# Gated linear attention in a two-layer decoder trunk: another sigmoid, one-region sums, half transposes, a second weight pool

## The chip, the cores and the metric

The kernel runs on one core of one Trainium2 chip. The metric is device time in microseconds (us) from launch to end on that core, the median of several runs; before the change three runs gave 2408.81, 2409.51 and 2409.78 us. Engines are named as in the profile: PE is the matrix engine (PEld its weight loads), DVE the vector engine, ACT the scalar engine, POOL the general one, SP the queue that issues the loads.

## What is computed

A decoder trunk of two layers over 272 tokens (16 learned meta tokens, then 256 real ones) with D_MODEL = 2048. Layer 0 mixes tokens with RWKV-7, layer 1 with gated linear attention (GLA); each is followed by an MLP with hidden size 8192. Everything is float32. The change touches layer 1's mixer alone:

```python
def gla_time_mix(x, w_in, w_a2, b_a, gn_w, w_o):        # x: (1, 272, 2048)
    p = x @ w_in                                        # q 1024 | k 1024 | v 2048 | gate 2048 | za 16
    glog = log_sigmoid(za @ w_a2 + b_a) / 16            # forget gate, per key dimension
    # 4 heads, key size 256, value size 512; chunks of 16 (meta) and then 64 tokens:
    #   b = cumsum(glog); q_t = q*exp(b); k_t = k*exp(-b)
    #   o = q_t @ S + tril(q_t @ k_t.T) @ v;  S = exp(b_last)*S + (k*exp(b_last - b)).T @ v
    o = o * rsqrt(mean(o*o, -1) + 1e-5) * gn_w          # per head
    return (o * silu(gate)) @ w_o                       # silu(g) = g * sigmoid(g)
```

## The kernel before

Activations lie transposed: 128 channels on the partitions, tokens along the free dimension. A weight matrix is cut into output tiles of 128 columns; the contraction over 2048 is two weight loads of 128x1024 floats (512 KB each), and each load serves eight steps of 128 (index `kt`, 0 to 15 over both loads). Products are made in three parts of a split float: `wload` (line 127) fetches a load into `raw` (3 buffers, DMA issued by SP), ACT writes its rounded copy `hi` (line 137), DVE the rest `lo = raw - hi` (line 138); `hi` and `lo` have 2 buffers each in the pool `wp`. The activations `x[kt]` have a high and a low half as well.

Two helpers multiply such a tile:

- `proj` (lines 160 to 162 in `mm3`) adds hi·xh, hi·xl and lo·xh for each step into one region of a PSUM bank: three matmuls, the sum is complete in PSUM.
- `projw` (lines 189 and 190) multiplies `hi` with both halves of x in one matmul of 512 columns (two regions of the bank), and `lo` with the high half in a second one of 256 columns. Two matmuls, but two regions are left to be added. `joined` (lines 199, 200) does that for the GLA's tiles: ACT copies one region into `cj`, DVE adds the other. `addto` (line 206) adds both regions into the residual on DVE.

`gla` (from line 987) first multiplies the 16-wide gate input, then runs over four heads. One head's tiles, in the order of PE: two query tiles (`projw` + `joined`, line 1047) and two key tiles (`proj` with 272 tokens, line 1059); then four value tiles (`proj`, line 1114), each transposed into token-major form by three fp32 transposes of 128x128 (line 1123) into one PSUM tile `pt` (2 buffers), copied out as `Vh` (ACT, line 1126) and `Vl` (DVE, line 1127); `weights` (line 1091) makes the chunk scores ahead of the first of them, `weigh(v)` (lines 1103, 1104) multiplies them with the values; then four gate tiles (`projw` + `joined`, line 1139). For each gate tile the sigmoid is made as exp(-g) (ACT, line 1148), plus one (ACT, line 1149), reciprocal (DVE, line 1150); `finish` multiplies it with the normalized output and splits the result into `oT`. A matmul with ones (line 1142) sums the squares for the head's norm behind the second gate tile; during gate tiles 1 and 2 of a head `gate` (line 1017 on PE) prepares the next head's forget gates. After the last head sixteen output tiles (line 1160) multiply `oT` with `gla_o`.

Each engine executes its instructions strictly in the order in which a scheduler wrote them when the program was built; weight loads carry a high priority there (`prio=2000`), so conversions stand as far ahead of their matmuls as the buffers allow. A conversion that waits for a free `hi` holds up all that stands behind it on ACT, and a DVE instruction that waits for ACT holds up the `lo` behind it.

## Time and profile before

| | |
|---|---|
| median of 3 runs | 2409.51 us (2408.81 to 2409.78) |
| profiled execution | 2414.07 us, of it 2412.3 us from the first to the last instruction |
| mean granted PE clock | 0.995 of full speed |
| GLA in the profiled execution | from about 1333 us to the first output tile at 1640 us, output tiles until about 1728 us |
| bytes read from HBM | 433.86 MB |

Times in the profile count from the first instruction. A row of a group of instructions names line, engine, operation, out<-in by the program's names, shape and count, then busy time and the mean of one in ns, then the idle time of that engine just before them and who ended it. In the timeline a row has start and duration; matmuls overlap, so the step between two starts is what one costs, not the duration of one. In a table of stretches each row has the stretch, its length, busy time and instruction count of each engine, the granted PE clock and the DMA share.

### The profile page before, as it was taken

The page shows a single profiled execution, that of the slowest core. Times are in us where ns is not written, and L with a number is a line of the kernel's source. Part 1 is how long each engine was busy: PE and PEld are TensorE (multiplying, and loading weights), DVE is VectorE, ACT ScalarE, POOL GpSimd, SP SyncE. Part 2 cuts the span into 40 slices and gives each one's busy share as a digit, 9 for nine tenths or more (in the row PEclk, how much of TensorE's full clock was granted, in tenths as well). Part 3 has the DMA queues.
Part 4 walks back from the last instruction along what each step waited for, and adds up shares of the span by engine and source line. Part 5 has one row for each costly group of instructions (what it writes and reads, how often), then busy time and mean ns, then how long its engine had stood idle before and what let it go on. Part 6 is the DMA issues. An engine that isn't in the chain of part 4 may idle for free.

```text
span 2412.3 us, 47144 instructions
## 1 busy us (share of the span) xinstructions
PE 2364.2 (98%) x19257; PEld 2233.8 (93%) x19257; DVE 1636.8 (68%) x2742; ACT 1239.3 (51%) x1951; POOL 6.6 (0%) x20
## 2 busy tenths in 40 slices
PE   9999999899999999999999999999999999999998
PEld 8888888789999999999999989998999999999997
DVE  8777886858655555555556788778766666666666
ACT  6366544456555445445445565545555545445444
POOL 0000000000000000000000000000000000000000
PEclk9999999999999999999999999999999999999999
DMA  6578765534555655555555554555666666666665
GB/s 211 170 233 284 240 191 147 148 88 155 183 192 188 190 191 189 188 191 192 187 190 192 182 172 161 166 166 180 197 201 201 201 202 201 202 201 201 201 201 172
DMA packets 160729, 455.29 MB, mean 189 GB/s; under 512 B 34112, under 2 KB 50624, under 8 KB 160512
## 3 DMA queue, kind: packets, MB, share of 16 engines
q1 hardware_dynamic: 160512, 452.27, 58.2%
q8 instruction: 151, 2.47, 0.4%
q14 instruction: 66, 0.54, 0.1%
HBM read 433.86 MB, written 18.35 MB: 187 GB/s over the span
## 4 chain that ended last, share of the span: by engine, by line
PE 70%; DVE 3%; ACT 1%; issue 0%; DVEq 0%; ACTq 0%
PE pj L189 23%; PE pj L160 12%; PE pj L162 12%; PE pj L161 12%; PE pj L190 11%; DVE lo L138 1%; PE pt L1091 0%; DVE sg L1150 0%; ACT hi L137 0%; PE pu L1103 0%; PE pt L1123 0%; DVE cum L1027 0%; DVE fin L1213 0%; PE pu L1104 0%; DVE cj L200 0%
## 5 line engine op out<-in xcount | busy, mean ns | idle before, releaser
L137 ACT CAST hi<-raw 128x1024 fp32r<-128x1024 f32 (+1 forms) x818 | 794.5, 979 | 951.4 <-PE pj L161 514.9
L138 DVE TENSOR_TENSOR lo<-raw,hi 128x1024 fp32r<-128x1024 f32 (+1 forms) x818 | 926.5, 1139 | 518.8 <-ACT hi L137 510.2
L160 PE MATMUL pj<-x,hi 128*128 128x272 f32 x2240 | 642.0, 287 | 5.7 <-DVE cj L200 4.0
L162 PE MATMUL pj<-x,lo 128*128 128x272 f32 x2240 | 629.1, 281 | 4.6 <-DVE lo L138 4.3
L161 PE MATMUL pj<-x,hi 128*128 128x272 f32 x2240 | 628.3, 280 | 0.2 <-DVE x L233 0.2
L189 PE MATMUL pj<-x,hi 128*128 128x512 f32 x1664 | 550.0, 384 | 2.3 <-DVE cj L200 1.3
L190 PE MATMUL pj<-x,lo 128*128 128x256 f32 x1664 | 455.8, 274 | 2.3 <-DVE lo L138 2.2
L160 PEld LDWEIGHTS pj<-x,hi 128*128 128x128 f32 x2240 | 424.2, 189 | 13.7 <-issue 3.7
L162 PEld LDWEIGHTS pj<-x,lo 128*128 128x128 f32 x2240 | 424.4, 189 | 8.0 <-DVE lo L138 7.3
L161 PEld LDWEIGHTS pj<-x,hi 128*128 128x128 f32 x2240 | 424.5, 190 | 3.6 <-issue 1.4
L189 PEld LDWEIGHTS pj<-x,hi 128*128 128x128 f32 x1664 | 315.4, 190 | 46.0 <-ACT hi L137 2.9
L189 PE MATMUL pj<-h,hi 128*128 128x512 f32 x1008 | 330.3, 382 | 0.0
L190 PEld LDWEIGHTS pj<-x,lo 128*128 128x128 f32 x1664 | 320.1, 192 | 6.8 <-DVE lo L138 6.3
L160 PE MATMUL pj<-h,hi 128*128 128x272 f32 (+1 forms) x1040 | 290.1, 279 | 0.0
L161 PE MATMUL pj<-h,hi 128*128 128x272 f32 (+1 forms) x1040 | 290.1, 279 | 0.0
L162 PE MATMUL pj<-h,lo 128*128 128x272 f32 (+1 forms) x1040 | 290.1, 279 | 0.0
L190 PE MATMUL pj<-h,lo 128*128 128x256 f32 x1008 | 274.8, 273 | 0.0
L189 PEld LDWEIGHTS pj<-h,hi 128*128 128x128 f32 x1008 | 190.5, 189 | 26.4
L160 PEld LDWEIGHTS pj<-h,hi 128*128 128x128 f32 x1040 | 196.6, 189 | 0.0
L161 PEld LDWEIGHTS pj<-h,hi 128*128 128x128 f32 x1040 | 196.6, 189 | 0.0
L162 PEld LDWEIGHTS pj<-h,lo 128*128 128x128 f32 x1040 | 196.6, 189 | 0.0
L190 PEld LDWEIGHTS pj<-h,lo 128*128 128x128 f32 x1008 | 193.5, 192 | 0.0
(268 smaller groups left out, 2110.5 us busy)
## 6 DMA issues: line engine op xcount, KB each, us to landing
raw<-mlp_w_d SPq DMA_DIRECT2D x512, 512.0 KB, 4.2
raw<-gla_in_d SPq DMA_DIRECT2D x98, 512.0 KB, 3.4
raw<-w_rkv_d SPq DMA_DIRECT2D x80, 512.0 KB, 4.1
raw<-gla_o_d SPq DMA_DIRECT2D x32, 512.0 KB, 4.2
raw<-w_r_d SPq DMA_DIRECT2D x16, 512.0 KB, 3.4
raw<-rw_oQ_d SPq DMA_DIRECT2D x16, 512.0 KB, 3.4
ard<-ar SPq DMA_DIRECT2D x16, 288.0 KB, 3.6
bkd<-bk SPq DMA_DIRECT2D x16, 288.0 KB, 4.3
```

What stands on the lines that cost most here:

```text
L137: nc.scalar.copy(hi[:, h], raw[:, h])
L138: nc.vector.tensor_tensor(out=lo[:, h], in0=raw[:, h], in1=hi[:, h].bitcast(F32), op=ALU.subtract)
L160: nc.tensor.matmul(out, hi[:, ws], xh, start=first, stop=False)
L161: nc.tensor.matmul(out, hi[:, ws], xl, start=False, stop=False)
L162: nc.tensor.matmul(out, lo[:, ws], xh, start=False, stop=last)
L189: nc.tensor.matmul(wide, hi[:, ws], xt, start=kt == 0, stop=False)
L190: nc.tensor.matmul(one, lo[:, ws], xt[:, 0], start=False, stop=kt == nk - 1)
```

## The change

```diff
@@ Kern.__init__
         self.raw_bufs, self.hi_bufs = 3, 2
         self.split_parts = 1
+        self.wps = [self.wp]
@@ wload
             raw = self.t(self.wp, [P, 1024], "raw", self.raw_bufs)
             nc.sync.dma_start(raw, src)
-            hi = self.t(self.wp, [P, 1024], "hi", self.hi_bufs, F32R)
-            lo = self.t(self.wp, [P, 1024], "lo", self.hi_bufs, F32R)
+            pool = self.wps[0]
+            self.wps = self.wps[1:] + [pool]
+            hi = self.t(pool, [P, 1024], "hi", self.hi_bufs, F32R)
+            lo = self.t(pool, [P, 1024], "lo", self.hi_bufs, F32R)
@@ projw
     def projw(self, srcs, x, off=0):
+        return self.projws([srcs], x, off)[0]
+
+    def projws(self, tiles, x, off=0):
         nc = self.nc
-        ps = self.pj()
-        wide, one = ps.rearrange("p (s t a) -> p s t a", s=2, a=2), self.pairs(ps[:, :SEQ])
-        nk = 8 * len(srcs)
-        for i, s in enumerate(srcs):
-            hi, lo = self.wload(s)
-            for j in range(8):
-                kt = 8 * i + j
-                ws = slice(j * P, (j + 1) * P)
-                xt = x[kt][:, :, off : off + SEQ].rearrange("p s (a t) -> p s t a", a=2)
-                nc.tensor.matmul(wide, hi[:, ws], xt, start=kt == 0, stop=False)
-                nc.tensor.matmul(one, lo[:, ws], xt[:, 0], start=False, stop=kt == nk - 1)
-        return self.back(ps[:, :SEQ]), self.back(ps[:, SEQ:])
+        pss = [self.pj() for _ in tiles]
+        nk = 8 * len(tiles[0])
+        for i in range(len(tiles[0])):
+            for ps, srcs in zip(pss, tiles):
+                wide, one = ps.rearrange("p (s t a) -> p s t a", s=2, a=2), self.pairs(ps[:, :SEQ])
+                hi, lo = self.wload(srcs[i])
+                for j in range(8):
+                    kt = 8 * i + j
+                    ws = slice(j * P, (j + 1) * P)
+                    xt = x[kt][:, :, off : off + SEQ].rearrange("p s (a t) -> p s t a", a=2)
+                    nc.tensor.matmul(wide, hi[:, ws], xt, start=kt == 0, stop=False)
+                    nc.tensor.matmul(one, lo[:, ws], xt[:, 0], start=False, stop=kt == nk - 1)
+        return [(self.back(ps[:, :SEQ]), self.back(ps[:, SEQ:])) for ps in pss]
@@ gla
         gp = es.enter_context(tc.tile_pool(name="gla", bufs=1, side="right", reuse_waits="tile"))
+        self.wps.append(es.enter_context(tc.tile_pool(name="wp2", bufs=1)))
...
-                pq = self.joined(gp, self.projw(pair(j), x, NMETA))
+                pq = self.proj(pair(j), x, SEQ, NMETA)
...
-                pt = self.ptr()
+                pts = [self.ptr(), self.ptr()]
                 for s, a in enumerate((0, c1, c2)):
-                    nc.tensor.transpose(pt[:, s * P : (s + 1) * P], vs[:, a : a + P], self.ident)
-                vc = slice(v * P, (v + 1) * P)
-                p3 = pt[:, : 3 * P].rearrange("p (s v) -> p s v", s=3)
-                nc.scalar.copy(Vh[:, :, vc], p3)
-                tt(Vl[:, :, vc], p3, Vh[:, :, vc].bitcast(F32), ALU.subtract)
+                    for q in range(2):
+                        half = slice(HEAD * q, HEAD * q + HEAD)
+                        nc.tensor.transpose(pts[q][:, s * HEAD : (s + 1) * HEAD], vs[half, a : a + P], self.ident[half, half])
+                for q in range(2):
+                    vc = slice(v * P + HEAD * q, v * P + HEAD * q + HEAD)
+                    p3 = pts[q][:, : 3 * HEAD].rearrange("p (s v) -> p s v", s=3)
+                    nc.scalar.copy(Vh[:, :, vc], p3)
+                    tt(Vl[:, :, vc], p3, Vh[:, :, vc].bitcast(F32), ALU.subtract)
...
-                pg = self.joined(gp, self.projw(pair(32 + 4 * hd + v), x, NMETA))
+                pg = self.proj(pair(32 + 4 * hd + v), x, SEQ, NMETA)
...
                 sg = self.t(gp, [P, SEQ], "sg", 2)
-                nc.scalar.activation(sg, gt, AF.Exp, scale=-1.0)
-                nc.scalar.activation(sg, sg, AF.Identity, bias=1.0)
-                nc.vector.reciprocal(out=sg, in_=sg)
+                nc.scalar.activation(sg, gt, AF.Abs)
+                nc.scalar.activation(sg, sg, AF.Exp, scale=-1.0)
+                nc.scalar.activation(sg, sg, AF.Ln, bias=1.0)
+                nc.vector.scalar_tensor_tensor(out=sg, in0=gt, scalar=0.0, in1=sg, op0=ALU.min, op1=ALU.subtract)
+                nc.scalar.activation(sg, sg, AF.Exp)
                 tt(gt, gt, sg)
...
+        out = lambda f: [ap["gla_o"][f, i] for i in range(2)]
+        first = self.projws([out(0), out(1)], oT)
         for f in range(KT):
-            self.addto(hres[:, f, NMETA:], self.projw([ap["gla_o"][f, i] for i in range(2)], oT))
+            self.addto(hres[:, f, NMETA:], first[f] if f < 2 else self.projw(out(f), oT))
             done(f)
+        self.wps = [self.wp]
         es.close()
```

The sigmoid is now exp(min(g, 0) - ln(1 + exp(-|g|))). In the changed file lines stand some lines further down: `lo` is line 141, `hi` line 140, `projw`'s matmuls 196 and 197, the transposes 1133, the sigmoid 1159 to 1163.

How the order of instructions moves is shown at three places. First DVE, where the last head's gate tiles 2 and 3 end and the output tiles begin. Before (`gt_20280` is gate tile 3; `lo_20317` and `lo_20384` are the second loads of output tiles 0 and 1, `lo_20362` is the first load of tile 1):

```order
L138 TENSOR_TENSOR lo_20317<-raw_20314,hi_20316 128x1024
L989 TENSOR_TENSOR gt_20221<-gt_20221,sg_20223 128x256
L200 TENSOR_TENSOR cj_20277<-pj_20232,cj_20277 128x256
L989 TENSOR_TENSOR gt_20221<-gt_20221,o_19695 128x256
L138 TENSOR_TENSOR lo_20362<-raw_20359,hi_20361 128x1024
L989 TENSOR_TENSOR x_16717<-gt_20221,x_16717 128x256
L989 TENSOR_TENSOR gt_20280<-cj_20277,acc_16624 128x256
L1131 SCALAR_TENSOR_TENSOR o_19695<-o_19695,vecs_126,hr_20155 128x256
L1150 RECIPROCAL sg_20282<-sg_20282 128x256
L989 TENSOR_TENSOR gt_20280<-gt_20280,sg_20282 128x256
L989 TENSOR_TENSOR gt_20280<-gt_20280,o_19695 128x256
L138 TENSOR_TENSOR lo_20384<-raw_20381,hi_20383 128x1024
```

and now (`gt_20721` is gate tile 3; `lo_20783` and `lo_20805` are the second loads of output tiles 0 and 1, `lo_20857` and `lo_20879` the loads of output tile 2, `x_16721` is the last part of `oT`):

```order
L1162 SCALAR_TENSOR_TENSOR sg_20649<-gt_20647,sg_20649 128x256
L141 TENSOR_TENSOR lo_20783<-raw_20780,hi_20782 128x1024
L996 TENSOR_TENSOR gt_20647<-gt_20647,sg_20649 128x256
L996 TENSOR_TENSOR gt_20647<-gt_20647,o_20054 128x256
L996 TENSOR_TENSOR gt_20721<-pj_20660,acc_16624 128x256
L141 TENSOR_TENSOR lo_20805<-raw_20802,hi_20804 128x1024
L996 TENSOR_TENSOR x_16720<-gt_20647,x_16720 128x256
L1162 SCALAR_TENSOR_TENSOR sg_20723<-gt_20721,sg_20723 128x256
L141 TENSOR_TENSOR lo_20857<-raw_20854,hi_20856 128x1024
L996 TENSOR_TENSOR gt_20721<-gt_20721,sg_20723 128x256
L996 TENSOR_TENSOR gt_20721<-gt_20721,o_20054 128x256
L141 TENSOR_TENSOR lo_20879<-raw_20876,hi_20878 128x1024
```

The conversion that stands behind the last sigmoid was one of output tile 1 and is now one of tile 2, and the addition of the two regions (`cj`) is gone.

Second PE, where the output tiles begin, now (`pj_20734` is output tile 0, `pj_20735` tile 1; `hi_20738`, `hi_20760`, `hi_20782`, `hi_20804` are the four loads; `x_16721` is step 15):

```order
L197 MATMUL pj_20734<-x_16713,lo_20739 128x256
L196 MATMUL pj_20735<-x_16706,hi_20760 128x512
...
L197 MATMUL pj_20735<-x_16713,lo_20761 128x256
L196 MATMUL pj_20734<-x_16714,hi_20782 128x512
...
L196 MATMUL pj_20735<-x_16714,hi_20804 128x512
L196 MATMUL pj_20734<-x_16721,hi_20782 128x512
```

Tile 0 stops after its first eight steps, tile 1 does its first eight, and only then the second halves follow; before, tile 0 went on to step 13 first and its steps 14 and 15 stood within tile 1.

Third PE, the transposes of a value tile other than a head's first, now (before there is one row here, three transposes into one `pt`):

```order
L1133 MATMUL pt_17223<-cst_125,vs_17210 128x64
L1133 MATMUL pt_17224<-cst_125,vs_17210 128x64
L1133 MATMUL pt_17223<-cst_125,vs_17210 128x64
L1133 MATMUL pt_17224<-cst_125,vs_17210 128x64
L1133 MATMUL pt_17223<-cst_125,vs_17210 128x64
L1133 MATMUL pt_17224<-cst_125,vs_17210 128x64
```

They alternate between the two halves of the partitions and between two PSUM tiles. For a head's first value tile the order is two, two, one, one.

## The prediction

> **What bounds the kernel now.** I read the page's busy times first, then who PE waits for inside GLA, then a table of stretches cut at fixed places of PE's order, then the steps of single tiles.
>
> ```profile
> PE 2364.2 (98%) x19257; PEld 2233.8 (93%) x19257; DVE 1636.8 (68%) x2742; ACT 1239.3 (51%) x1951; POOL 6.6 (0%) x20
> ```
>
> PE is busy 98% of the span, so a gain can only come from PE's work itself or from the gaps in it. PE's own waits from 1333 to 1656 us (who waits, for whom, total, times, longest):
>
> ```profile
> PE pj L160 <- DVE cj L200: 4.0, 3, 1.6
> PE pj L190 <- DVE lo L138: 2.2, 6, 0.9
> PE pj L189 <- DVE cj L200: 1.3, 1, 1.3
> PE pj L189 <- ACT hi L137: 1.0, 1, 1.0
> ```
>
> Almost all of them name DVE: either the bank that `joined` has not yet freed, or a `lo` that comes late. Idle time understates the loss, because a matmul that waited starts with an empty pipeline. So I price by lengths. These stretches run from a head's norm matmul (L1142) to the next head's scores (L1091), with one value part (L1091 to L1142) as second row; the last one runs from the last L1142 to the first matmul of output tile 2.
>
> ```profile
> 1399.54:1442.42 42.88, 39.78 (x279) 36.80 (x278) 41.58 (x90) 27.11 (x49) 0.00 (x0) 1.00 0.54 172
> 1442.42:1477.02 34.60, 34.60 (x270) 33.51 (x269) 21.33 (x34) 16.72 (x28) 0.00 (x0) 1.00 0.46 153
> 1477.02:1518.39 41.37, 39.68 (x279) 36.62 (x277) 39.81 (x85) 24.92 (x43) 0.00 (x0) 1.00 0.56 178
> 1552.99:1593.71 40.72, 39.09 (x277) 36.45 (x276) 38.38 (x80) 22.79 (x37) 0.00 (x0) 1.00 0.55 181
> 1628.32:1655.08 26.76, 24.48 (x132) 20.89 (x131) 24.33 (x38) 14.65 (x25) 0.00 (x0) 0.94 0.49 160
> ```
>
> In the value part DVE is busy 21.3 of 34.6 us and PE has no gap. In the three gate stretches DVE (fourth number) is busy 97, 96 and 94%, and there PE stalls. What they would take without a stall follows from undisturbed tiles: one `proj` tile of 272 tokens, one `projw` tile, and the program's very last tile, which is a `proj` of 256 tokens:
>
> ```profile
> 1588.15:1593.71 5.56, 5.56 (x50) 5.56 (x49) 4.18 (x12) 2.09 (x2) 0.00 (x0) 1.00 0.59 188
> 2389.59:2394.83 5.24, 5.24 (x34) 4.82 (x33) 3.64 (x5) 3.00 (x4) 0.00 (x0) 1.00 0.31 109
> 2394.83:2400.19 5.36, 5.36 (x50) 5.36 (x49) 2.41 (x4) 1.95 (x3) 0.00 (x0) 1.00 0.00 0
> ```
>
> The short matmuls between the tiles, from the timeline (start, duration; the step to the next start counts):
>
> ```profile
> 1477.02 0.60 PE L1142 MATMUL pry<-oacc,cst 128*128 128x256 f32 x2
> 1477.27 0.57 PE L189 MATMUL pj<-x,hi 128*128 128x512 f32 x1
> ...
> 1483.29 0.29 PE L1017 MATMUL pm<-za,wa 128*128 128x272 f32 x1
> 1483.42 0.38 PE L189 MATMUL pj<-x,hi 128*128 128x512 f32 x1
> ```
>
> A gate stretch holds two gate tiles, two query tiles, two key tiles and a value tile: 4 x 5.24 + 3 x 5.56 + 0.25 + 2 x 0.13 = 38.15 us. It takes 42.88, 41.37 and 40.72, so 4.7 + 3.2 + 2.6 = 10.5 us are stalls. The last stretch holds two gate tiles and two output tiles, 0.25 + 4 x 5.24 = 21.2 us, and takes 26.76: 5.5 us. Together **16.0 us** of stalls. The last stretch has its own reason, seen on DVE and PE:
>
> ```profile
> 1646.72 1.75 DVE L1150 RECIPROCAL sg<-sg 128x256 f32<-128x256 f32 x1 [0.53 <-ACT sg L1149]
> ...
> 1649.30 1.22 DVE L138 TENSOR_TENSOR lo<-raw,hi 128x1024 fp32r<-128x1024 f32 x1
> ```
> ```profile
> 1653.47 0.63 PE L189 MATMUL pj<-x,hi 128*128 128x512 f32 x1
> ...
> 1654.11 0.63 PE L189 MATMUL pj<-x,hi 128*128 128x512 f32 x1
> ```
>
> The `lo` of output tile 1 stands behind the last sigmoid's reciprocal, PE waits for it, and then a step of `projw` takes 0.64 us instead of 5.24/16 = 0.33: the row of the stretch shows a granted clock of 0.94, half speed for a while after the gaps. About 1.6 of the 5.5 us are that clock.
>
> **The change part by part.**
>
> *Sums in one region.* Sixteen gate and eight query tiles go from 5.24 to 5.36 us on PE: 24 x 0.12 = **+2.9 us**, all on PE's path. In exchange ACT loses 24 copies and DVE 24 additions, and PSUM banks come free after one DVE instruction instead of an ACT and a DVE one:
>
> ```profile
> L1150 DVE RECIPROCAL sg<-sg 128x256 f32<-128x256 f32 x16 | 28.0, 1749 | 1.9 <-ACT sg L1149 1.9
> L200 DVE TENSOR_TENSOR cj<-pj,cj 128x256 f32<-128x256 f32 x24 | 10.0, 417 | 0.0
> ...
> L1050 DVE SCALAR_TENSOR_TENSOR qf<-cj,acc 128x256 f32<-128x256 f32 x8 | 3.4, 422 | 0.1
> ```
> ```profile
> L199 ACT COPY cj<-pj 128x256 f32<-128x256 f32 x24 | 8.7, 363 | 0.0
> ...
> L1148 ACT ACTIVATE sg<-gt 128x256 f32<-128x256 f32 x16 | 6.7, 416 | 2.5 <-DVE gt L989 2.5
> ```
>
> The columns streamed are the same, 768 a step; only one more matmul is issued. The Trainium skill, "TensorE: Matmul & The Clock Gate", section "Back-to-back issue gap", has N/2.4 ns plus about 2.5 ns for each warm matmul. By that the extra one would cost 2.5 ns in 24 x 16 steps, an estimate of 1.0 us, and the sum would be 1.9 us better; the two tiles above show 2.9, and the measured tile decides.
>
> *Sigmoid.* Per gate tile DVE loses 1.749 us and gains one two-step instruction of about 0.42 (L1050's form); ACT goes from two activations to four, +0.83. No new function table should be needed: `gate` already uses the absolute value, exp and ln between the same instructions.
>
> *DVE and ACT then.* A gate stretch holds three sigmoids and five sums: DVE loses 3 x 1.33 + 5 x 0.42 = 6.1 us, the second one falls from 39.8 of 41.4 us to 33.7 of 39 (86%). ACT gains 3 x 0.83 - 5 x 0.36 = 0.7 us, to 25.6 of 39 (66%). Neither is full.
>
> *Weight buffers.* Four pairs of `hi` and `lo` instead of two: PE may run 4 x 2.7 = 10.7 us on converted loads instead of 5.4 (half of a 5.36 tile each). It adds no instruction. The three gate stretches need bridging of 3 to 5 us at most, so this alone would cover them; it costs nothing as long as loads keep coming, and the DMA engines are busy 0.54 to 0.56 of those stretches.
>
> *Output tiles in pairs.* Step 15 of tile 0 is now needed 8 + 8 + 7 steps, 23 x 0.33 = 7.5 us, after the last gate tile. The chain that makes it: three activations, one DVE instruction, a `hi` that stands between (1.05 us), the last activation, two products, a `lo` (1.2), a cast and a subtraction, by the durations above 7 to 8 us. So it is about on time, and a few tenths may be left. The conversions of tiles 0 and 1 now stand ahead of the last sigmoid, and without a gap there is no half clock.
>
> *What stays of the stalls.* The loss per stretch falls from 4.7 to 2.6 us while DVE's share falls from 97 to 94%, so at 86% it should be gone; I leave 0.5 us in each of the four stretches, **2.0 us** in all, between 0.5 (only the chain into step 15) and 6.
>
> *Transposes in halves.* Three fp32 transposes of 128 columns become six of 64 rows and 64 columns, which alternate between two halves of the array. Before, and in RWKV the nearest forms, pairs in two halves (L518):
>
> ```profile
> 1597.83 0.49 PE L1123 MATMUL pt<-cst,vs 128*128 128x128 f32 x3
> ...
> 1598.27 0.28 PE L161 MATMUL pj<-x,hi 128*128 128x272 f32 x1
> ```
> ```profile
> 331.05 0.28 PE L162 MATMUL pj<-x,lo 128*128 128x272 f32 x1
> 331.26 1.15 PE L518 MATMUL pt<-AR,BK 64*64 64x64 f32 x32
> 332.34 0.38 PE L160 MATMUL pj<-x,hi 128*128 128x272 f32 x1
> 332.56 0.28 PE L161 MATMUL pj<-x,hi 128*128 128x272 f32 x1
> ```
> ```profile
> 256.22 1.16 PE L518 MATMUL pt<-AR,BK 64*128 64x128 f32 x8
> 257.30 0.38 PE L160 MATMUL pj<-x,hi 128*128 128x272 f32 x1
> ```
>
> An ordinary step is 5.56/48 = 0.12 us. The three old transposes cost 1598.27 - 1597.83 - 0.12 = 0.32. The 16 pairs of L518 last 1.08, 0.068 a pair, but the step into them is 0.21 and the first one behind them 0.22, so each visit to the halved array costs 0.19 extra. Three pairs: 0.19 + 0.2 = 0.39, and about 0.45 with the first and the last pair, which overlap with nothing on one side; against 0.32 that is +0.13, times 16 value tiles **+2.1 us**. Lower bound: no extra visit cost, 0.2 instead of 0.33, -2.1 us. Upper bound: the halves do not pair, as in the group at 256.22, where 8 last 1.08, 0.135 each: 0.19 + 0.81 = 1.0, +10 us. The order alternates like L518's pairs, so I take +2.1. The Trainium skill speaks against this edit: "TensorEngine Tiling (Array Packing)", section "Key Properties", says that changing the tiling mode drains the engine. The steps of 0.21 and 0.22 agree with it. By its table of theoretical speedups, up to 2x for a contraction of 64, the edit would give at most half of 0.33 x 16, an estimate of 2.6 us of gain, and the sum would be 4.7 us better; the row of L518 decides. The copies out of PSUM become twice as many and half as long; DVE and ACT have 13 and 18 us free in each value part.
>
> **Sum.** -16.0 + 2.0 + 2.9 + 2.1 = -9.0 us. The profiled execution took 2414.07 us, its span 2412.3, so the changed span should be about 2403.3. The runs' median lies 4.6 us below the profiled execution; the same gain on it gives **2400.5 us**.
>
> **Rivals.**
>
> - *Half of the stalls stay* (8 us), because ACT now has four activations a gate tile and a `hi` stands between the third and the fourth, so a gate tile's chain crosses between ACT and DVE twice more. For it: in the last stretch DVE did wait 0.53 us for ACT. Against it: ACT at 66%. Time: 2409.5 - 16.0 + 8 + 2.9 + 2.1 = 2406.5.
> - *The stalls stay whole and the change is slower.* The place is DVE's queue in the gate part: a product that waits for the last activation holds up the `lo` behind it, the activation waits behind a `hi`, and that `hi` waits for PE to free its buffer. If that ring runs at PE's pace, two more buffers do not help. Price: nothing gained, 2.9 + 2.1 paid, 2414.5. It decides from 11 us of stalls left. Against it: in the new order the conversions stand two loads further ahead of the sigmoids.
> - *The transposes do not pair*: +10 instead of +2.1, 2408.4. For it: a head's first value tile has the order two, two, one, one, and L518 has groups of both speeds.
> - *All goes well*: 0.5 us of stalls left and the transposes at their lower bound: -16.0 + 0.5 + 2.9 - 2.1 = -14.7, 2394.8.
>
> **How the numbers follow.** Chances: forecast 0.64, half of the stalls 0.14, slower 0.07, unpaired 0.05, all well 0.10. The forecast's own spread comes from the stalls left (0.5 to 6) and the transposes (-2 to +6): 2395 to 2408.5. The range 2394 to 2409 takes in all but the slower case and some of the ends. A measurement of this kernel can tell about 0.2%, 4.8 us: faster means below 2404.7, slower above 2414.3. Faster: 0.61 of the forecast, 0.10, 0.05 of the half-stalls case and 0.01: 0.77. Slower: 0.06 of the slower case and 0.01 of ends: 0.07. Same: 0.16.
>
> **What would show it.** In the changed profile the value part should last 34.60 + 2 x 0.12 + 4 x 0.13 = 35.4 us; over 37 means unpaired transposes, under 34.9 paired ones without a visit cost. A gate stretch should last 38.15 + 4 x 0.12 = 38.6 plus at most 0.5, with DVE near 86%; if it stays at 41 the stalls were not DVE's. The last stretch should last about 22 us with a granted clock of 1.00. A tile of 256 tokens should take 5.36 us. RWKV and both MLPs should not move; if they do, or if PE's waits in GLA name ACT's `hi` for many us, the prediction is wrong.

## The result and the profile after

The changed kernel takes 2400.75 us (median of five runs, 2398.74 to 2402.54), the kernel before 2409.78 us beside it: a ratio of 0.996, 95% interval 0.9949 to 0.997. It is 9.0 us faster. A second set of runs of the same two kernels gave 2401.99 against 2410.26 us, a ratio of 0.9965 (0.9953 to 0.9977).

The page's first part after the change (busy time, share, instructions):

```profile
span 2400.8 us, 48047 instructions
PE 2360.9 (98%) x19689; PEld 2244.1 (93%) x19689; DVE 1611.9 (67%) x2734; ACT 1242.4 (52%) x1975; POOL 6.6 (0%) x20
```

PE has 432 matmuls more (24 tiles x 16 steps for the sums, 48 for the transposes), yet its busy time is 3 us lower: busy time holds half-clock stretches and the slow starts behind a wait too, and does not show what the edits cost. So the lengths of the stretches are read, as in the prediction. The table of stretches after the change, with the columns as before (from:to, length, busy time of PE, PEld, DVE, ACT and POOL with counts, granted clock, DMA share, GB/s): one value part, two gate stretches, the last stretch.

```profile
1363.18:1398.64 35.46, 35.46 (x314) 34.71 (x313) 21.40 (x38) 17.36 (x33) 0.00 (x0) 1.00 0.43 149
1398.64:1437.45 38.81, 38.81 (x342) 38.76 (x341) 33.71 (x77) 24.77 (x44) 0.00 (x0) 1.00 0.54 190
1472.91:1511.72 38.81, 38.81 (x343) 38.76 (x342) 33.71 (x77) 24.78 (x44) 0.00 (x0) 1.00 0.56 191
1621.49:1643.50 22.01, 21.90 (x164) 20.73 (x163) 18.17 (x32) 15.45 (x28) 0.00 (x0) 1.00 0.55 192
```

The gate stretches have lost their idle time and their scatter: 38.81 us each in place of 42.88, 41.37 and 40.72, with DVE at 33.7 us. The last stretch went from 26.76 to 22.01 us at a clock of 1.00. The value parts pay: 35.46 in place of 34.60. Who PE still waits for, from the window 1325 to 1345 us, where GLA begins (waiter, releaser, total, times, longest); the prediction's window, 1333 to 1656 us, has only the second and the third of these rows, so the view shows no wait of PE in the gate part any more:

```profile
PE pm L255 <- DVE acc L251: 1.3, 1, 1.3
PE pm L1025 <- DVE za L996: 0.6, 1, 0.6
PE pm L1025 <- DVE mn L1032: 0.5, 1, 0.5
PE pj L165 <- DVE lo L141: 0.5, 1, 0.5
```

The same window of the kernel before has only two rows:

```profile
PE pm L248 <- DVE acc L244: 0.4, 1, 0.4
PE pm L1017 <- DVE za L989: 0.2, 1, 0.2
```

So a new loss stands at GLA's entrance, which the prediction did not have. The balance of the layer is seen in two long stretches: from RWKV's last transposes (568 us before, 564 after; called RWKV's end below) to the first head's norm matmul, and from there to GLA's end, which is the first matmul of the norm that follows the output tiles. Before, then after:

```profile
567.97:1399.54 831.57, 829.57 (x7081) 825.72 (x7080) 498.26 (x665) 396.22 (x543) 0.00 (x0) 1.00 0.58 188
1399.54:1731.62 332.08, 323.20 (x2229) 301.32 (x2228) 267.37 (x478) 182.35 (x298) 0.00 (x0) 0.99 0.54 173
```
```profile
563.64:1398.64 835.00, 830.93 (x7157) 828.22 (x7156) 499.67 (x669) 398.53 (x548) 0.00 (x0) 1.00 0.55 188
1398.64:1719.40 320.76, 320.57 (x2583) 310.65 (x2581) 240.81 (x464) 182.19 (x316) 0.00 (x0) 1.00 0.52 178
```

Behind the first norm matmul 11.3 us are won, ahead of it 3.4 us are lost: 7.9 us in this execution, and 8.8 us in the one of the second set (834.06 and 320.75). Of the difference between the two profiled executions another 4.3 us lie ahead, in RWKV, whose instructions the change does not touch.

### The profile page after: what moved, and what is told of

It is laid out like the page before. It is cut to its first block, busy times and chain, and to the rows that moved or that the text cites. A ratio compares the mean times of both kernels' runs of the same rounds, so it can differ in the third digit from the quotient of the medians.

```text
span 2400.8 us, 48047 instructions
## 1 busy us (share of the span) xinstructions
PE 2360.9 (98%) x19689; PEld 2244.1 (93%) x19689; DVE 1611.9 (67%) x2734; ACT 1242.4 (52%) x1975; POOL 6.6 (0%) x20
## 5 line engine op out<-in xcount | busy, mean ns | idle before, releaser
L163 PE MATMUL pj<-x,hi 128*128 128x272 f32 (+1 forms) x2624 | 748.6, 285 | 1.7 <-DVE hres L300 1.0
L165 PE MATMUL pj<-x,lo 128*128 128x272 f32 (+1 forms) x2624 | 734.5, 280 | 4.3 <-DVE lo L141 4.1
L164 PE MATMUL pj<-x,hi 128*128 128x272 f32 (+1 forms) x2624 | 734.0, 280 | 0.2 <-DVE x L240 0.2
L163 PEld LDWEIGHTS pj<-x,hi 128*128 128x128 f32 x2624 | 498.1, 190 | 10.2 <-issue 3.7
L164 PEld LDWEIGHTS pj<-x,hi 128*128 128x128 f32 x2624 | 498.2, 190 | 3.6 <-issue 1.4
L196 PE MATMUL pj<-x,hi 128*128 128x512 f32 x1280 | 419.9, 382 | 0.1
L197 PE MATMUL pj<-x,lo 128*128 128x256 f32 x1280 | 348.8, 273 | 0.0
L196 PEld LDWEIGHTS pj<-x,hi 128*128 128x128 f32 x1280 | 241.9, 189 | 34.1 <-DVE x L996 0.4
```

Of the source, the lines that this page charges most:

```text
L163: nc.tensor.matmul(out, hi[:, ws], xh, start=first, stop=False)
L164: nc.tensor.matmul(out, hi[:, ws], xl, start=False, stop=False)
L165: nc.tensor.matmul(out, lo[:, ws], xh, start=False, stop=last)
L196: nc.tensor.matmul(wide, hi[:, ws], xt, start=kt == 0, stop=False)
L197: nc.tensor.matmul(one, lo[:, ws], xt[:, 0], start=False, stop=kt == nk - 1)
```

## The experiments

Twelve kernels ran. The whole times of one kernel lie 3 to 9 us apart from the lowest to the highest, so each verdict below rests on the lengths of stretches, which repeat to 0.1 us from head to head and from execution to execution wherever PE has no stall. All are cut as above: the value part from a head's scores to its norm matmul, the gate stretch from there to the next head's scores, the last stretch up to output tile 2. "From the norm" is the long stretch from the first norm matmul to GLA's end. Each ratio is to runs of the kernel before made beside that kernel (medians of 2409.78 to 2410.59 us), so the times of two rows compare less well than their lengths.

| kernel | time, us | ratio to before (95%) | value | gate stretches | last | from the norm |
|---|---|---|---|---|---|---|
| before | 2409.78 | 1 | 34.60 | 42.88, 41.37, 40.72 | 26.76 | 332.08 |
| after | 2400.75 | 0.9949–0.997 | 35.46 | 38.81 x3 | 22.01 | 320.76 |
| after, again | 2401.99 | 0.9953–0.9977 | 35.47 | 38.81 x3 | 22.01 | 320.75 |
| full transposes | 2399.16 | 0.9938–0.9965 | 34.84 | 38.81 x3 | 22.01 | 318.83 |
| two-region sums | 2401.57 | 0.9941–0.9966 | 35.22 | 38.33 x3 | 22.07 | 318.63 |
| one pool | 2405.46 | 0.9967–0.9984 | 35.46 | 39.78 x3 | 22.01 | 324.28 |
| old sigmoid | 2408.39 | 0.9982–1.0 | 35.57 | 41.20, 38.78, 41.20 | 22.73 | 326.55 |
| single output tiles | 2401.56 | 0.9949–0.9974 | 35.46 | 38.81 x3 | 22.05 | 320.82 |
| single tiles, one pool | 2405.69 | 0.9973–0.9991 | 35.47 | 39.77 x3 | 23.30 | 325.74 |
| halves in series | 2402.75 | 0.9961–0.9981 | 35.49 | 38.81 x3 | 22.01 | 320.79 |
| before + pool | 2409.73 | 0.9986–1.0004 | 34.60 | 42.18, 40.49, 40.49 | 24.30 | 327.24 |
| before + sigmoid | 2403.19 | 0.9958–0.9981 | 34.60 | 39.72 x3 | 24.06 | 323.45 |
| best | 2397.63 | 0.9933–0.9958 | 34.60 | 38.33 x3 | 22.08 | 316.79 |
| best, pool later | 2396.68 | 0.9933–0.9958 | 34.61 | 38.33 x3 | 22.07 | 316.79 |

**Full transposes.** The changed kernel with the old transposes:

```diff
-                pts = [self.ptr(), self.ptr()]
+                pt = self.ptr()
                 for s, a in enumerate((0, c1, c2)):
-                    for q in range(2):
-                        half = slice(HEAD * q, HEAD * q + HEAD)
-                        nc.tensor.transpose(pts[q][:, s * HEAD : (s + 1) * HEAD], vs[half, a : a + P], self.ident[half, half])
...
+                    nc.tensor.transpose(pt[:, s * P : (s + 1) * P], vs[:, a : a + P], self.ident)
...
```

The copies out of PSUM are the old ones again, too.

> The changed kernel with the three full fp32 transposes of 128 columns in place of the six halves; all else as changed. Theory A (the halves cost PE time at their borders, 0.155 us a group): a value part lasts 35.46 - 4 x 0.155 = 34.84 us, the gate stretches stay at 38.8 us, and the time falls by 16 x 0.155 = 2.5 us, to about 2398.3 us. Rival (the value part grew for another reason, such as the sums or the activations beside it): it stays above 35.2 us and the time within 1 us of 2400.75. Second rival (the halves save PE work): a value part over 35.6 us and a slower kernel.

The value part is 34.84 us, exactly theory A's figure. The time of 2399.16 us is 1.6 lower in place of the 2.5 of theory A, within what runs scatter. Where the 0.155 us a group goes is seen in PE's timeline, first with halves, then with full transposes (start, duration; only steps between starts count):

```profile
1446.98 0.25 PE L1112 MATMUL pu<-A,Vl 128*128 128x64 f32 x1
1447.16 0.40 PE L1133 MATMUL pt<-cst,vs 64*128 64x64 f32 x6
1447.49 0.38 PE L163 MATMUL pj<-x,hi 128*128 128x272 f32 x1
1447.71 0.28 PE L164 MATMUL pj<-x,hi 128*128 128x272 f32 x1
```
```profile
1445.17 0.24 PE L1112 MATMUL pu<-A,Vl 128*128 128x64 f32 x1
1445.25 0.55 PE L1131 MATMUL pt<-cst,vs 128*128 128x128 f32 x3
1445.55 0.36 PE L163 MATMUL pj<-x,hi 128*128 128x272 f32 x1
1445.75 0.28 PE L164 MATMUL pj<-x,hi 128*128 128x272 f32 x1
```

The step into the group is 0.18 us in place of 0.08, six halves take 0.33 in place of 0.30 for three full ones, and the first step behind them is 0.22 in place of 0.20: 0.73 against 0.58 us. In a head's first value tile the three full ones take 0.25 and the six halves 0.33, so there the group loses 0.20 us; the mean of a head's four is 0.155. The halves stream half the columns each, but there are twice as many of them, so they take no less time (0.33 against 0.30 us), and the visit has to be paid for. The Trainium skill, "TensorEngine Tiling (Array Packing)", section "Key Properties", says that a change of tiling mode drains the engine; the longer step at the group's entry, 0.10 us, agrees with it.

**Halves in series.** Is it the alternation that lets six halves pass in 0.33 us?

```diff
-                for s, a in enumerate((0, c1, c2)):
-                    for q in range(2):
+                for q in range(2):
+                    for s, a in enumerate((0, c1, c2)):
```

> The changed kernel with the six half transposes of a value tile ordered three of the upper half, then three of the lower, in place of alternating halves; all else as changed. Theory A (alternating halves run in pairs, 0.33 us for six, and the 0.155 us a group is lost at the borders with the whole-array matmuls): without neighbours to pair with, six take about 0.11 us each, 0.66 in place of 0.33, so a value part lasts up to 4 x 0.33 = 1.3 us more, 36.4 to 36.8 us, and the time rises by 4 to 5 us to about 2405. Rival (there is no pairing, a half transpose simply takes half of a full one, and the loss is six starts in place of three): value parts stay at 35.3 to 35.6 us and the time at 2400.75 within 1 us.

```profile
1364.92:1400.41 35.49, 35.49 (x315) 34.74 (x313) 21.40 (x38) 17.36 (x33) 0.00 (x0) 1.00 0.46 150
```

A value part takes 35.49 us, 0.03 more than with alternating halves. The rival has the number; the order of the six does not matter. Whether the two halves of the array work side by side in either order, or a half transpose just takes half of a full one, this run cannot tell.

**Two-region sums.** Query and gate sums as before, the rest as changed:

```diff
-                pq = self.proj(pair(j), x, SEQ, NMETA)
+                pq = self.joined(gp, self.projw(pair(j), x, NMETA))
...
-                pg = self.proj(pair(32 + 4 * hd + v), x, SEQ, NMETA)
+                pg = self.joined(gp, self.projw(pair(32 + 4 * hd + v), x, NMETA))
```

> The changed kernel with query and gate sums in two regions of a bank again (the sum of the halves made by an ACT copy and a DVE addition); all else as changed. Theory A (the buffers and the cheaper sigmoid end the stalls, and the one region only costs PE 0.12 us a tile): gate stretches of 38.2 to 38.6 us, value parts of 35.2, the time 24 x 0.12 = 2.9 us lower, about 2397.9. Rival (the one-region sums ended the stalls, since they free the bank early and take 24 additions from DVE): gate stretches of 39.5 to 41.5 us, PE waiting on DVE's cj again, and the time 2401 to 2408.

```profile
1364.56:1399.79 35.23, 35.23 (x283) 33.64 (x281) 20.54 (x37) 17.21 (x33) 0.00 (x0) 1.00 0.46 150
1399.79:1438.12 38.33, 38.33 (x279) 36.58 (x277) 36.16 (x85) 26.72 (x50) 0.00 (x0) 1.00 0.61 193
```

The gate stretch is 38.33 us with PE busy throughout, although DVE is back at 36.16 us, 94% of it. So the one-region sums are not what ended the stalls, and 94% of DVE is no stall by itself. They cost 0.24 us a value part and 0.48 us a gate stretch; in the last stretch, with two gate tiles in it, nothing is seen (22.01 against 22.07). From the norm matmul on that is 2.1 us. The time, 2401.57 us, did not follow: from RWKV's end to GLA's end the profiled execution is 3 to 4 us shorter than the two of the changed kernel, but its RWKV part ended 2 to 3 us later. Why the median did not fall stays open; the runs lie between 2397.32 and 2401.97.

**One pool.** The changed kernel without the second pool:

```diff
-        self.wps.append(es.enter_context(tc.tile_pool(name="wp2", bufs=1)))
```

> The changed kernel with one pool of two hi and two lo buffers as before; all else as changed. Theory A (DVE's full queue made the stalls, and the smaller load alone ends them): gate stretches of at most 39.3 us with DVE near 86%, the new stall of 1.6 us at the entrance of GLA gone (first GLA matmul to first scores 34.9 us instead of 36.5), the time 2399 to 2402. Rival (the buffers end the stalls): gate stretches of 40 to 42 us with PE waiting for hi and lo, and the time 2403 to 2410.

```profile
1401.81:1441.59 39.78, 39.43 (x343) 39.02 (x342) 33.84 (x77) 24.69 (x44) 0.00 (x0) 1.00 0.57 186
```

Between the two theories: 0.97 us a gate stretch come back, PE waits for `lo` again (1.4 us in all), and the output tiles behind the last stretch take 0.64 us more (76.54 against 75.90). The buffers are worth 3 x 0.97 + 0.64 = 3.5 us.

**Old sigmoid.** The changed kernel with exp, an addition of one and the reciprocal in the gate:

```diff
-                nc.scalar.activation(sg, gt, AF.Abs)
-                nc.scalar.activation(sg, sg, AF.Exp, scale=-1.0)
-                nc.scalar.activation(sg, sg, AF.Ln, bias=1.0)
-                nc.vector.scalar_tensor_tensor(out=sg, in0=gt, scalar=0.0, in1=sg, op0=ALU.min, op1=ALU.subtract)
-                nc.scalar.activation(sg, sg, AF.Exp)
+                nc.scalar.activation(sg, gt, AF.Exp, scale=-1.0)
+                nc.scalar.activation(sg, sg, AF.Identity, bias=1.0)
+                nc.vector.reciprocal(out=sg, in_=sg)
```

> The changed kernel with the old sigmoid (exp, an addition of one on ACT, a reciprocal of 1.75 us on DVE); all else as changed. Theory A (DVE's load made the stalls): gate stretches of 39.5 to 41 us with DVE over 93%, the last stretch 23 to 25 us, the time 2403 to 2408. Rival (the buffers bridge any wait of DVE, as the prediction said): gate stretches stay within 0.3 us of 38.8 and the time within 1.5 us of 2400.75.

```profile
1400.29:1441.49 41.20, 39.54 (x342) 39.12 (x342) 38.76 (x82) 25.60 (x44) 0.00 (x0) 1.00 0.55 180
1477.09:1515.87 38.78, 38.78 (x340) 38.73 (x340) 35.20 (x72) 20.86 (x32) 0.00 (x0) 1.00 0.58 190
1551.45:1592.64 41.19, 39.40 (x341) 39.00 (x341) 37.24 (x77) 23.39 (x38) 0.00 (x0) 1.00 0.55 180
```

The rival falls, and theory A holds in kind, with the middle stretch and the last (22.73) below its ranges. 2.2 us of the gain are left (2408.39 against 2410.59 us of the kernel before beside it, the interval just reaching 1.0), with two pools and one-region sums in place. Two of the three stretches stall by 2.4 us, the middle one, with fewer DVE and ACT instructions in it, does not. The buffers do not bridge this wait: the first gate stretch shows the bank as its cause,

```profile
1419.38 0.35 PE L163 MATMUL pj<-x,hi 128*128 128x272 f32 x1 [1.50 <-DVE gt L996]
```

a matmul that has its weights and waits for the DVE instruction that reads the previous sums out of the bank.

**Before + pool.** The kernel before with only the second pool:

```diff
+        self.wps = [self.wp]
...
-            hi = self.t(self.wp, [P, 1024], "hi", self.hi_bufs, F32R)
-            lo = self.t(self.wp, [P, 1024], "lo", self.hi_bufs, F32R)
+            pool = self.wps[0]
+            self.wps = self.wps[1:] + [pool]
+            hi = self.t(pool, [P, 1024], "hi", self.hi_bufs, F32R)
+            lo = self.t(pool, [P, 1024], "lo", self.hi_bufs, F32R)
...
+        self.wps.append(es.enter_context(tc.tile_pool(name="wp2", bufs=1)))
...
```

> The kernel before with nothing but the second pool of two hi and two lo buffers for GLA. The prediction said that this alone would cover the stalls: gate stretches of 38.2 to 38.7 us instead of 42.9, 41.4 and 40.7, and a time about 10 us lower, 2399 to 2401. Rival (DVE at 94 to 97% of the gate part was the limit, and buffers cannot make it faster): gate stretches of 40 to 42 us, PE still waiting for cj, at most 4 us gained, 2405 to 2410; the entrance of GLA 1.5 us longer than before here too.

```profile
1399.50:1441.68 42.18, 38.92 (x279) 36.76 (x278) 41.41 (x90) 27.10 (x49) 0.00 (x0) 1.00 0.52 174
1476.27:1516.77 40.50, 38.57 (x279) 36.64 (x278) 39.65 (x85) 25.04 (x43) 0.00 (x0) 1.00 0.53 182
```

The rival holds. The median does not move (2409.73 us, interval to 1.0004), and the gate stretches lose 0.2 to 0.9 us where the prediction's statement wanted 2.4 to 4.5. (The profiled lengths add up to a little more than the median: from RWKV's end to GLA's end 1160.0 us against 1163.65, of which some 1.7 are the half clock in the last stretch of the old execution, below.) The waits of PE in GLA tell why the gate part keeps its length:

```profile
PE pj L163 <- DVE cj L207: 5.6, 3, 2.1
PE pj L196 <- ACT dec L1044: 1.7, 1, 1.7
```

The waits for `hi` and `lo` that stood in this view before (1.0 and 2.2 us) are gone, but those for the bank, which `cj` frees, have grown. The row that names ACT's `dec` is one of them:

```profile
1412.48 0.45 PE L196 MATMUL pj<-x,hi 128*128 128x512 f32 x1 [1.65 <-ACT dec L1044]
```
```profile
1411.92 0.42 DVE L207 TENSOR_TENSOR cj<-pj,cj 128x256 f32<-128x256 f32 x1
```

A matmul does not use `dec`, which ended only 0.02 us ahead of it. `cj` ended 0.14 us ahead of it, as in the other waits for the bank (0.15 us below), and the kernel before has a wait of 1.28 us for `cj` at the same place. So the bank waits are 5.6 + 1.7 = 7.3 us, against 4.0 + 1.3 = 5.3 before. PE's longest wait in the second gate stretch, and DVE's timeline ahead of it:

```profile
1494.77 0.35 PE L163 MATMUL pj<-x,hi 128*128 128x272 f32 x1 [1.93 <-DVE cj L207]
```
```profile
1487.95 1.75 DVE L1158 RECIPROCAL sg<-sg 128x256 f32<-128x256 f32 x1
...
1492.12 1.22 DVE L141 TENSOR_TENSOR lo<-raw,hi 128x1024 fp32r<-128x1024 f32 x1
1493.25 0.42 DVE L996 TENSOR_TENSOR x<-gt,x 128x256 fp32r<-128x256 f32 x1
1493.59 0.72 DVE L1035 TENSOR_TENSOR_SCAN cum<-gc,mn 128x272 f32<-128x272 f32 x1
1494.22 0.40 DVE L207 TENSOR_TENSOR cj<-pj,cj 128x256 f32<-128x256 f32 x1
```

No row has idle time before it: DVE works through its queue, a `lo` that nobody waits for yet among it, and `cj` is late because the queue ahead of it is. PE goes on 0.15 us after `cj` ends. The last stretch became 2.5 us shorter, and the half clock that it no longer has is the larger part of that.

**Before + sigmoid.** The kernel before with only the new sigmoid, the edit of "old sigmoid" the other way round.

> The kernel before with nothing but the new sigmoid (four activations and one DVE instruction in place of two activations and a reciprocal). Theory A (DVE's load made the stalls): DVE falls by 3 x 1.33 = 4 us in a gate stretch, the stretches last 38.3 to 39.5 us, the value parts 34.6 us, the last stretch 23 to 25 us, and the time is 2398 to 2402. Rival (the late freeing of banks by the joined sums made them): stretches of 40 to 42 us, PE waiting on cj, the time 2405 to 2409.

```profile
1397.67:1437.39 39.72, 39.21 (x279) 36.67 (x278) 36.16 (x85) 26.84 (x50) 0.00 (x0) 1.00 0.56 186
```
```profile
PE pj L197 <- DVE lo L141: 1.0, 5, 0.2
PE pj L165 <- DVE lo L141: 0.8, 3, 0.3
PE pj L196 <- ACT hi L140: 0.8, 2, 0.5
```

Theory A in kind, though 39.72 us and 2403.19 us lie just above its ranges: this edit alone takes 1.0 to 3.2 us out of each gate stretch, 2.7 out of the last (some 1.7 of them the half clock of the old execution), and 7.2 us off the median (2403.19 against 2410.35 beside it). What is left, 1.4 us a stretch above 38.33, are waits for `hi` and `lo` alone; no row names `cj`. Here the second pool helps, as the two-region run shows.

**Single output tiles**, with two pools and with one:

```diff
-        first = self.projws([out(0), out(1)], oT)
         for f in range(KT):
-            self.addto(hres[:, f, NMETA:], first[f] if f < 2 else self.projw(out(f), oT))
+            self.addto(hres[:, f, NMETA:], self.projw(out(f), oT))
```

> The changed kernel with output tiles 0 and 1 one after the other as before; all else as changed. Theory A (with single tiles, step 15 of output tile 0 comes 8 steps, some 2.6 us, earlier than the last product can be ready, so PE stands and its clock falls): the last stretch 24 to 27 us instead of 22.0, with a granted clock below 1.00 there, the gate stretches at 38.8, the time 2403 to 2406. Rival (the reciprocal behind which the conversion stood was the whole cause, and four buffers hold the weights ready): the last stretch 22 to 23 us, the time within 1.5 us of 2400.75.

> The changed kernel with neither the second pool nor the pairing of output tiles; the new sigmoid, the one-region sums and the halves stay. Taking away one of the two left the last stretch at 22.0 us. Theory A (either of them is enough once the sigmoid is short, because both put the weights of output tiles 0 and 1 ahead of the last sigmoid): without both it lasts 23.5 to 24.5 us, as with the new sigmoid alone (24.06), the gate stretches 39.8 as with one pool. Rival (the short sigmoid and the one-region sums are enough): 22.0 to 22.5 us.

```profile
1623.47:1646.77 23.30, 22.41 (x165) 20.73 (x164) 18.56 (x32) 15.45 (x28) 0.00 (x0) 1.00 0.53 178
```

With two pools the pairing is worth nothing: 22.05 us, the rival of the first expectation. The row is the last stretch with one pool: without the second pool it is worth 1.3 us of the last stretch (23.30 against 22.01). The second expectation's theory A holds in kind, a little below its range: pairing and buffers do the same work there, and either is enough.

**Best.** Old sums and transposes, new sigmoid, paired tiles, and the second pool opened behind the first two `gate` calls; then the same with the pool opened still later:

```diff
         for j in range(2):
             gate(j)
+        self.wps.append(es.enter_context(tc.tile_pool(name="wp2", bufs=1)))
```

> The changed kernel without the two edits that were found to cost PE time (full transposes and two-region sums again), and with the second pool of buffers opened only behind the first two gates of GLA, past its entrance. If the costs of sums (2.9 us), transposes (2.5) and entrance (1.6) are separate and the buffers with the new sigmoid suffice for the gate part: value parts of 34.6 us, gate stretches of 38.2 to 38.6, the entrance 34.7, the last stretch 21.7, and 2393 to 2395 us. If the one-region sums are needed to keep the gate part free of stalls: gate stretches of 39.5 to 41 and 2396 to 2402.

```diff
-        self.wps.append(es.enter_context(tc.tile_pool(name="wp2", bufs=1)))
...
+            if hd == 0:
+                self.wps.append(es.enter_context(tc.tile_pool(name="wp2", bufs=1)))
+
             def weights():
```

> The best kernel so far (two-region sums, full transposes, new sigmoid, paired output tiles, second pool) with the pool opened still later, in front of the first head's value tiles. In the best kernel a wait of 0.7 us for the second gate was left at the entrance. Theory A (the conversions that fill the new buffers stand ahead of the gate's work on ACT and DVE): RWKV's end to GLA's first scores 797.0 us as before the change, instead of 797.6, no wait over 0.3 us at the gates' matmuls, the rest as in the best kernel, about 0.6 us gained. Rival (that wait has other causes): 797.6 us again. In both cases gate stretches of 38.33 and 2396 to 2398 us.

> The changed kernel itself once more, on the same chip as the best kernel's variant, to compare the two without the spread between chips. Lengths as before: value parts 35.46, gate stretches 38.81, last stretch 22.01 us. Its time should be 4 to 6 us above the best kernel's by the lengths (4 x 0.86 + 3 x 0.48 us in value parts and gate stretches, and up to 1.9 at the entrance), 2400 to 2403 us.

The first version's two long stretches, then the second's:

```profile
560.96:1393.17 832.21, 829.84 (x7081) 825.85 (x7080) 499.23 (x666) 398.55 (x546) 0.00 (x0) 1.00 0.57 189
1393.17:1709.96 316.79, 316.56 (x2227) 299.53 (x2225) 246.84 (x476) 188.49 (x326) 0.00 (x0) 1.00 0.55 180
```
```profile
561.37:1395.38 834.01, 830.13 (x7082) 825.95 (x7080) 499.33 (x666) 398.39 (x546) 0.00 (x0) 1.00 0.59 188
1395.38:1712.17 316.79, 316.57 (x2227) 299.57 (x2225) 246.81 (x476) 188.48 (x326) 0.00 (x0) 1.00 0.55 180
```

From the norm matmul on both are 4.0 us shorter than the changed kernel. Up to it, the first version loses 0.6 us against the kernel before, the second 2.4: the later opening did not help, since PE now waits 0.9 us for a `hi` and 0.8 us for a `lo` at the place where the pool opens. ACT's conversions there had themselves stood 3.19 us for a load to land. Theory A of that run falls. The medians are 2397.63 and 2396.68 us. On one chip the second version took 2396.68 (2394.96 to 2400.26) and the changed kernel 2401.99 us (2399.11 to 2403.94): 5.3 us for undoing two of the five edits and opening the pool later. The 2393 to 2395 expected of the first version was not met in the median. Its lengths from RWKV's end to GLA's end give 14.7 us against the kernel before, its median 12.7.

## Why the prediction was right, and where not

The forecast was 2400.5 us, the result 2400.75. The mechanism of the largest term was right; that the total agrees to 0.3 us is luck, since the sum of -9.0 us came out by errors that cancel, and the runs of the changed kernel alone lie 3.8 us apart.

- **Stalls, -16.0 + 2.0.** The mechanism was right: PE's stalls in the gate part came from DVE's queue (the new sigmoid alone ends all but 1.4 us of each), and they are gone at 38.81 us, the predicted 38.6 plus 0.2. Free of stalls a stretch with two-region sums takes 38.33 us (measured), not 38.15; by that the old stalls were 4.55 + 3.04 + 2.39 = 10.0 us rather than 10.5. All of these went, where 0.5 a stretch were left in the sum; in the last stretch 0.6 us remain. The term is -15.0 in place of -14.0, again from the lengths with the cost of the sums put back (3 x 0.48 + 0.24).
- **Sums in one region, +2.9.** Confirmed in the value parts and gate stretches: 0.12 us a tile. In the last stretch it does not show; the cost of its two tiles is put back in the sum above all the same. That they also relieve the stalls turned out to matter only without the second pool: 39.78 us with one-region sums against 39.72 without, so 0.48 paid and 0.42 won. Here they are a pure cost.
- **Weight buffers: "this alone would cover them".** This step was wrong. The run with only the pool gained nothing that the median shows, and its gate stretches stayed at 40.5 to 42.2 us. The argument added up all waits into microseconds of bridging, but PE waited for two things: converted weights, which a deeper buffer brings, and a free PSUM bank, which only an earlier DVE instruction brings. The old waits view had said so: 5.3 us stood against `cj`, 3.2 against `hi` and `lo`, in the rows of the prediction. The error did not reach the sum, because the sigmoid was in the same change. "It costs nothing as long as loads keep coming" did not hold at the entrance, where ACT waited for loads; see below.
- **DVE's share as the measure of stalls.** "At 86% it should be gone" gave the right answer by a wrong rule: at 94% with two-region sums there is no stall either, and with the old sigmoid there are stalls of 2.4 us at 94 and 90%. Two things count. One is DVE's work against PE's: the first two old gate stretches held 41.58 and 39.81 us of it against 38.33 of PE's, and while it stands there (41.41 and 39.65 us with only the pool) no buffer brings them to 38.33. The other is how late the instruction that frees the bank stands: the third old stretch (38.38 us of DVE's work) and the two with the old sigmoid (38.76 and 37.24 against 38.81) lose 2.4 us though DVE's work is not or hardly more than PE's, and the 1.75 us reciprocal is the longest block in the queue ahead. No run separates the two.
- **Output tiles in pairs.** The last stretch came out at 22.01 us as forecast, at a clock of 1.00, but not through the pairing: with two pools it does nothing. The new sigmoid alone takes 2.7 of the 4.75 us (to 24.06), the one-region sums 0.8 (to 23.30, single tiles and one pool), and pairing or buffers the last 1.3.
- **Transposes in halves, +2.1.** Measured 16 x 0.155 = 2.5. Most of the cost is at the group's entry, 0.10 us; the exit, which the prediction counted like the entry, costs only 0.02 more than behind full transposes, and the six halves themselves take 0.03 more than the three full ones (0.08 in a head's first value tile). The part of the argument about pairs is not supported: six took 0.33 us where three pairs at L518's pace were to take 0.2, and their order plays no role. The upper bound of +10 came from a row with 128 moving columns (64x128), twice the columns of this edit's.
- **Not in the sum.** The entrance. From RWKV's end to the first norm matmul, with the measured costs of sums and transposes taken off, the eight executions with the pool open from GLA's start take 1.1 to 2.4 us longer than the kernel before (the changed kernel 2.3 and 1.4), the two with one pool and one-region sums 0.8 and 0.6, the one with only the new sigmoid 0.0. A part of it is lost ahead of the norm matmul at GLA's start (L255): PE reaches it 0.9 to 2.4 us later than in the six executions without the pool there, but 0.7 of that are six more matmuls of 0.116 us that now stand ahead of it. The rest goes in the waits for `za` and `mn` behind it. ACT's and DVE's rows suggest how: with free buffers a conversion goes onto ACT's queue before its load has landed and holds up what stands behind it. In the changed kernel ACT stood 2.2 and 1.7 us for loads shortly before, and `acc` ended late behind `wa`, which stood behind `acc` before. No run isolates this. And not in the sum on the other side: the output tiles behind the last stretch gain 0.64 us from the buffers.

Together: -15.0 + 2.9 + 2.5 - 0.6 + 1.4 to 2.3 for the entrance, that is -8.8 to -7.9, against medians of -9.0 and -8.3. Of the rivals, half of the stalls staying and ACT as the new bound are excluded by the waits view, in which ACT does not appear; unpaired transposes by the value part. RWKV and the two MLPs kept their instructions; RWKV's length moved all the same, along with the granted clock, as below.

## What to carry to other kernels

Sort the waits of the bounding engine by what they wait for before pricing a remedy: here more weight buffers removed waits for weights only, and the waits for a PSUM bank ended when the instruction that empties it came earlier in its queue. Take the edits of a bundle apart even where the bundle wins: here the sigmoid alone gives 7 us, the pool alone moves no median and gains 3.5 us beside the sigmoid (less what it costs at the entrance), two edits cost 5 us together and one does nothing beside the pool. A deeper buffer is filled where it opens, and what it lets run early stands in the same queues as the chain that is due there.

## What the runs showed of the hardware

- The unchanged RWKV part ended between 561.0 and 568.3 us in the fourteen profiled executions, and the granted clock goes along with it: in the three executions with 3.4 us of half clock in that part it ended at 561.0, 561.4 and 563.3 us, in the three with 13.7 us at 566.7, 568.0 and 568.3. From the first norm matmul to GLA's end, two executions of the changed kernel agreed to 0.01 us. Effects of 2 us are read in stretches, not in the whole time.
- One more matmul for the same 768 columns costs 7.5 ns a step (0.12 us in 16), as the two-region run confirms. The Trainium skill, "TensorE: Matmul & The Clock Gate", section "Back-to-back issue gap", gives about 2.5 ns a matmul on top of its columns, for isolated warm matmuls; the measurement decides.
- Gaps of PE were followed by half clock at one place and not at others. The kernel before had gaps of 1.02 and 0.90 us in its last stretch and then 3.45 us at 0.51; the kernel with only the pool had gaps of 0.45 and 0.94 us there and stayed at 1.00, as it did behind its single gaps of 1.6 to 2.1 us in the gate stretches. What decides it these runs do not show. For each kernel PE's gaps in the timeline, then the stretch behind them with its clock (columns as in the other tables of stretches):

```profile
1649.20 0.48 PE L189 MATMUL pj<-x,hi 128*128 128x512 f32 x1 [1.02 <-ACT hi L137]
1650.58 0.38 PE L190 MATMUL pj<-x,lo 128*128 128x256 f32 x1 [0.90 <-DVE lo L138]
```
```profile
1651.30:1654.75 3.45, 3.45 (x14) 3.00 (x12) 2.47 (x4) 1.86 (x3) 0.00 (x0) 0.51 0.45 152
```
```profile
1648.91 0.48 PE L196 MATMUL pj<-x,hi 128*128 128x512 f32 x1 [0.45 <-DVE x L996]
1650.77 0.45 PE L196 MATMUL pj<-x,hi 128*128 128x512 f32 x1 [0.94 <-DVE hres L213]
```
```profile
1650.77:1655.00 4.23, 4.23 (x26) 3.88 (x27) 3.22 (x5) 2.82 (x6) 0.00 (x0) 1.00 0.64 200
```
